# First modulation pieces ahead of the sums of squares, first key norms beside the value products, and modulation matmuls and y transposes tied to program order

## The chip, the cores and the metric

The kernel is one program on one core of a Trainium2 chip. The metric is the device time of one execution in microseconds (us), as the median of several; the profile is that of one execution, taken by the hardware profiler. Names used below: PE is TensorE (matrix products), PEld its weight loads, DVE is VectorE, ACT is ScalarE, POOL is GpSimd, SP is SyncE, whose queue issues the DMAs.

## The reference, cut to what matters

Two blocks of two layers each run over 256 tokens and 256 context tokens of width 2048. The change lies mostly in the first layer of the first block and in the first layer of the second. Every layer modulates its input with vectors that come from a product of a condition with a 2048 x 6144 matrix:

```python
shift_l, scale_l, gate_l = jnp.split((sc @ mod_w[l] + mod_b[l])[:, None, :], 3, axis=-1)
shift_c, scale_c, gate_c = jnp.split(scc @ mod_w[l] + mod_b[l], 3, axis=-1)
```

The first layer is windowed attention: h is x divided by its root mean square (a sum of squares over the 2048 features of each token), scaled and shifted by the modulation, and q, k, v and a gate are products of h with one matrix; each head of q and k is normed, and for the latent tokens rotated, before the scores. The first layer of the second block holds a recurrence over heads of 64, computed in chunks of 64 tokens, whose output y is normed by chunk rows before it is scaled:

```python
mu = jnp.mean(y, -1, keepdims=True)
var = jnp.mean(jnp.square(y - mu), -1, keepdims=True)
yn = ((y - mu) * lax.rsqrt(var + GN_EPS)).reshape(B, T, RWKV_W) * gn_g + gn_b
```

## The kernel before, in words

All activations lie feature by token, 16 blocks of 128 features by 512 tokens (256 context, 256 latent). Products run in split precision: each operand is a high part (`hi`, made by ACT) and a low part (`lo`, the difference, made by DVE), and `mm3` issues three matmuls, hi by hi, hi by lo, lo by hi (lines 368 to 370). Weights stream from memory by `weights`: a DMA of two blocks (`raw`, line 354), then `split` into `whi` (ACT, line 339) and `wlo` (DVE, line 340); after each block of weights it calls `fill`.

`fill` is what sets the order of the side work. It holds generators with a rate each; at every call it adds the rate and runs as many steps as are owed. Two generators exist. `mod_steps` is the modulation: a step takes one loaded piece of modulation weights (`mraw`, 1 MB, by `mod_load`) and multiplies it with the conditions into one PSUM bank (`mv`, line 270); after a batch of pieces the sums are transposed back (line 286) and the bias is added (line 293). `mod_open` gives it a pool with a number of buffers and a rate for the stage, `mod_close` ends that, and `need` runs steps until the named column groups are done. `PACE` gives the rates, by stage: 0.3 in the windowed attention (swa), 0.5 in its output stage (x1), 0.2 in the second layer (mla), 0 in its output stage (x2), 0.25 in the recurrence stage (even), 0.5 in its output stage (x3). The other generator is `rwkv_units`: 16 units (8 head pairs by two directions), up to four at a time, one step of each active unit per `fill`.

The order in which each engine finally issues its instructions is made at compile time by a scheduler: it goes through the instructions in the order in which the program traced them, with priorities, and lets an instruction go ahead of others when it reckons its operands to be ready and an engine to be free. `keep_in_program_order(ins)` takes that freedom away: it puts an instruction behind the instruction traced before it on the same engine, in order of issue alone, with no wait. In `mod_steps` it stands on all matmuls of a piece but the first, so that a piece stays together, while its first matmul may move.

The first stage, in `tile_network`, goes so: x is loaded in four DMAs, ACT squares it and DVE sums the squares into `acc`; three modulation loads are issued; `rms_spread` makes the sums over features on PE (`tok_sums`, line 480), the power -1/2 on POOL (line 472) and a spread over partitions on PE (line 490). Then for each pair of feature blocks the modulation columns are run (`need`), the blocks of h are made by `put_h` (lines 510 to 516), and key products (`keys`, accumulators `kb`) and value products (`values`, banks `vp`) follow in pieces from the list `todo`. `gqa` comes after that stage: it loads norm rows, sine and cosine tables, then norms the four key tiles `kb[t]` (`head_norm`, lines 627 to 649, `late` and `feat` for the transposes to features, line 660, at most `VL` = 2 kept waiting) and starts the query products, whose four accumulators are those of the keys.

At the end of a unit, `rwkv` norms `y` (lines 1465 to 1476), transposes it in two banks of four transposes (`yt`, line 1487), and scales it.

Of the kernel before, what the change touches and what calls it, by code (L numbers as in the profile page):

```python
# [18 lines left out]
P = 128  # L19
# [41 lines left out]
VQ = 3  # L61
# [57 lines left out]
class Net:  # L119
# [129 lines left out]
    def mod_steps(self):  # L249
        nc = self.nc  # L250
        for i in range(4):
            if i % 2 == 0:
                self.conditions(i // 2)
            mod, cs = self.mod[i], self.cs
            for gs in MOD_BATCHES if i else MOD_FIRST:
                pb = self.bank("mv")
                half = isinstance(gs[0], tuple)
                nq, nk, cols = (2, 8, 256) if half else (4, 4, 512)
                for n, g in enumerate(gs):
                    for q in range(nq):  # L260
                        while len(self.mod_ahead) < (self.mod_pool[1] - 1 if self.mod_pool and self.mod_loads else 0):
                            self.mod_load()
                        if not self.mod_ahead:
                            self.mod_load()
                        raw = self.mod_ahead.pop(0)

                        for kk in range(nk):
                            k, j = nk * q + kk, kk % 4
                            with self.tc.high_priority(None if kk else 0):
                                mm = nc.tensor.matmul(  # L270
                                    pb[32 * j : 32 * j + 32, :cols], cs[:, 32 * k + 30 - 2 * n : 32 * k + 62 - 2 * n],
                                    raw[:, kk, :], start=(n == 0 and k < 4), stop=(n == len(gs) - 1 and k >= KD - 4),
                                    tile_position=(0, 32 * j),
                                )
                                if kk:
                                    self.tc.keep_in_program_order(mm)
                        self.mod_wait = MOD_LAG
                        yield
                ev = self.t512("ev", cols=cols)
                nc.scalar.copy(ev, pb[:, :cols])  # L280
                for _ in range(MV_LAG):
                    yield
                p2 = self.bank("mv2")
                c, nb = 2 * len(gs), cols // P
                for j in range(nb):
                    nc.tensor.matmul(
                        p2[:, c * j : c * j + c], ev[:, j * P : (j + 1) * P], self.sel[:, :c], start=True, stop=True
                    )
                for n, g in enumerate(gs):
                    o = g[0] * 4 + g[1] * 2 if half else g * 4  # L290
                    bias = self.v("mod_b", i * 48 + o, nb).unsqueeze(2).broadcast_to([P, nb, 2])
                    pv = p2[:, : nb * c].rearrange("p (j n c) -> p j n c", j=nb, c=2)[:, :, n, :]
                    nc.vector.tensor_tensor(mod[:, o : o + nb, :], pv, bias, op=ALU.add)
                    self.mod_done.add((i, g))
                    if half and g[1]:
                        self.mod_done.add((i, g[0]))
                yield
# [175 lines left out]

    def tok_sums(self, srcs, tiles, rhs):

        pb = self.bank("sums")
        w = rhs.shape[-1]
        for t in range(tiles):
            for n, src in enumerate(srcs):
                self.nc.tensor.matmul(  # L480
                    pb[:, t * w : (t + 1) * w], src[:, t * P : (t + 1) * P], rhs,
                    start=(n == 0), stop=(n == len(srcs) - 1),
                )
        return pb

# [12 lines left out]

    def rms_spread(self, acc, tiles):
        pb = self.tok_sums([acc], tiles, self.ones)  # L500
        rs = self.small(4, "rs")
# [183 lines left out]

    def gqa(self, w, windowed, kb, v=None):
        nc, I, h = self.nc, self.I, self.h
# [4 lines left out]
        with self.tc.tile_pool(name=pre, bufs=1) as ph:  # L692
            pt = v[2] if v else ph
            self.load_rows(pt, [pre + "_q", pre + "_qs", pre + "_k", pre + "_ks"] + (["sink"] if windowed else []))
            tq = self.rope_tables(pt, I[pre + "_cos"], I[pre + "_sin"], pre + "_q", pre + "_qs", P, pre + "q")
            tk = self.rope_tables(pt, I[pre + "_cos"], I[pre + "_sin"], pre + "_k", pre + "_ks", P, pre + "k")
            if windowed:
# [5 lines left out]
                nc.vector.tensor_copy(idr, self.ident)  # L703
            kh, kl = [pt.tile([P, 4, NT], F32R, name=n + pre) for n in ("kh", "kl")]
            vh, vl = v[:2] if v else [ph.tile([P, 4, 512], F32R, name=n + pre) for n in ("vh", "vl")]

            late = []

            def norm(t, ps, dst, tabs, g, base):

                rope = None if t < 2 else (tabs[0][:, t - 2, :], tabs[1][:, t - 2, :])
                q = self.head_norm(ps, 4, P, gain=self.row(g), rope=rope)
                s = slice(t * P - base, (t + 1) * P - base)
                late.append((q, 4, P, dst[0][:, :, s], dst[1][:, :, s]))

            def feat():
                if late:
                    self.to_feat(*late.pop(0))

# [6 lines left out]
            def q_job(g):  # L726
# [3 lines left out]
                for t in toks:  # L730
                    norm(t, banks[t], qs[g], tq, pre + "_q", q0)
                    if len(late) > QLATE[windowed]:
# [10 lines left out]

            for t in range(4):
                norm(t, kb[t], (kh, kl), tk, pre + "_k", 0)
                if v and len(late) > VL:
                    feat()
            if not v:
                vb = {}
# [5 lines left out]
            for n, _ in enumerate(q_job(0)):  # L755
                if v and n < 4 * VQ and n % VQ == VQ - 1:
                    feat()
# [434 lines left out]
    def rwkv(self, ph, b, d, pads, lora, yscr, sums):  # L1192
# [289 lines left out]
        for c0 in (0, 1):  # L1482
            pb = self.bank("yt")
            for n in range(4):
                c = 2 * n + c0
                src = y[:, c : c + 2, :].rearrange("p c t -> p (c t)") if c < NCH - 1 else yw
                nc.tensor.transpose(pb[:, n * P : (n + 1) * P], src, self.ident)
            pv = pb.rearrange("p (n t) -> p n t", n=4)
# [198 lines left out]
def tile_network(ctx, tc, I, out, dbg=None, stop=9):  # L1687
# [11 lines left out]
    with tc.tile_pool(name="x0", bufs=1) as px:  # L1699
# [7 lines left out]
        for _ in range(3):  # L1707
            N.mod_load()
        pr = N.rms_spread(acc, 4)
        rr = px.tile([P, NT], F32, name="rr0")  # L1710
# [13 lines left out]
        def values(g):  # L1724
# [11 lines left out]
            for t in range(4):  # L1736
# [13 lines left out]
                yield  # L1750

        kb = {}
        kgen = keys(kb)
        todo = []
        for g, u in ((g, u) for g in range(4) for u in range(2)):
# [16 lines left out]
            if u:  # L1772
                todo += [values(g)] * 16
        owed = 0.0
# [7 lines left out]
    N.dump("h0", h[0].bitcast(F32))  # L1782
    put_o = N.gqa(I["swa_in"], True, kb, (vh, vl, pV))
    pv.close()
# [33 lines left out]
    with tc.tile_pool(name="x2", bufs=1) as px:  # L1818
        xn = px.tile([P, KD, NT], F32, name="x2")
        N.more(px, XX[1], RX[3])  # L1820
        N.mod_open(px, 3, PACE[3])
        N.need(1, range(12))
# [26 lines left out]
        N.mm_feat(I["ev_lora"][0], h, KD, 256, LAT, [b[:, LAT] for b in lb])  # L1849
        N.mod_close()  # L1850
        N.dump("x2", xn)
# [210 lines left out]
```

## Time and profile before

| | us |
|---|---|
| median of 3 runs | 3263.63 (3262.27 to 3267.89) |
| the profiled execution, its time | 3252.14 |
| the profiled execution, its span (first to last instruction) | 3250.0 |
| mean granted TensorE clock in it | 0.981 |
| PE busy | 3080.6 (95%) |
| DVE busy | 2101.4 (65%) |
| ACT busy | 1481.1 (46%) |

Times of instructions are counted from the start of the span. A clock of 1.00 is 2.4 GHz, 0.50 is 1.2 GHz; a mean between them says that a stretch holds some of each. An engine that is idle costs time only where it is the one that everything else waits for.

### The profile page before, as it was taken

The page shows a single profiled execution, that of the slowest core. Times are in us where ns is not written, and L with a number is a line of the kernel's source. Part 1 is how long each engine was busy: PE and PEld are TensorE (multiplying, and loading weights), DVE is VectorE, ACT ScalarE, POOL GpSimd, SP SyncE. Part 2 cuts the span into 40 slices and gives each one's busy share as a digit, 9 for nine tenths or more (in the row PEclk, how much of TensorE's full clock was granted, in tenths as well). Part 3 has the DMA queues.
Part 4 walks back from the last instruction along what each step waited for, and adds up shares of the span by engine and source line. Part 5 has one row for each costly group of instructions (what it writes and reads, how often), then busy time and mean ns, then how long its engine had stood idle before and what let it go on. Part 6 is the DMA issues. An engine that isn't in the chain of part 4 may idle for free. (4 is left out here: it accounts for less than half of the span.)

```text
span 3250.0 us, 53765 instructions
## 1 busy us (share of the span) xinstructions
PE 3080.6 (95%) x20018; PEld 2399.4 (74%) x20018; DVE 2101.4 (65%) x4663; ACT 1481.1 (46%) x3237; POOL 347.7 (11%) x536
## 2 busy tenths in 40 slices
PE   6999999989988999999999999999999999899997
PEld 4667777767777878897776666766767768678887
DVE  3356455543476666665887788778877555857766
ACT  3324444442376666653334333433434424646664
POOL 0000000000001111000122222222221101200000
PEclk8999999999999999999999999999999999999999
DMA  8843444358654656766434434334445474443454
GB/s 309 319 158 130 149 139 153 137 185 283 232 168 136 229 195 230 258 224 204 142 95 150 127 110 133 98 105 148 124 130 161 165 269 141 161 143 130 143 180 152
DMA packets 270773, 556.10 MB, mean 171 GB/s; under 512 B 122928, under 2 KB 150704, under 8 KB 244912
## 3 DMA queue, kind: packets, MB, share of 16 engines
q1 hardware_dynamic: 270512, 552.68, 51.0%
q8 instruction: 157, 2.57, 0.3%
q14 instruction: 104, 0.85, 0.1%
HBM read 517.46 MB, written 35.13 MB: 170 GB/s over the span
## 5 line engine op out<-in xcount | busy, mean ns | idle before, releaser
L340 DVE TENSOR_TENSOR wlo<-raw,whi 128x512 fp32r<-128x512 f32 (+2 forms) x1000 | 660.5, 668 | 545.7 <-ACT whi L339 510.8
L368 PE MATMUL a<-hhi,whi 128*128 128x512 f32 (+1 forms) x2752 | 972.4, 354 | 16.6 <-ACT whi L339 12.1
L339 ACT CAST whi<-raw 128x512 fp32r<-128x512 f32 (+2 forms) x1000 | 592.7, 599 | 800.9 <-PE a L369 467.5
L369 PE MATMUL a<-hlo,whi 128*128 128x512 f32 (+1 forms) x2752 | 947.2, 345 | 0.3 <-DVE hlo L461 0.3
L370 PE MATMUL a<-hhi,wlo 128*128 128x512 f32 (+1 forms) x2752 | 939.8, 347 | 3.4 <-DVE wlo L340 3.1
L368 PEld LDWEIGHTS a<-hhi,whi 128*128 128x128 f32 x2752 | 524.9, 191 | 124.1 <-ACT whi L339 43.3
L370 PEld LDWEIGHTS a<-hhi,wlo 128*128 128x128 f32 x2752 | 522.1, 191 | 61.7 <-DVE wlo L340 8.4
L369 PEld LDWEIGHTS a<-hlo,whi 128*128 128x128 f32 x2752 | 525.6, 191 | 48.7 <-issue 4.5
L472 POOL TENSOR_TENSOR rs<-st,mhalf 128x4 f32<-128x4 f32 (+3 forms) x109 | 149.0, 1367 | 1660.8 <-DVE st L469 1632.9
L368 PE MATMUL a<-whi,hhi 128*128 128x512 f32 (+1 forms) x672 | 262.3, 401 | 15.9 <-ACT sq L629 6.4
L369 PE MATMUL a<-wlo,hhi 128*128 128x512 f32 (+1 forms) x672 | 264.6, 394 | 1.5 <-DVE wlo L340 1.3
L370 PE MATMUL a<-whi,hlo 128*128 128x512 f32 (+1 forms) x672 | 261.2, 391 | 0.0
L270 PE MATMUL mv<-mraw,cs 128*32 128x512 f32 (+1 forms) x1792 | 212.3, 562 | 16.2 <-DMA mraw<-mod_w 10.9
L1443 POOL TENSOR_SCALAR SD<-SV,DL 64x64 f32<-64x64 f32 x224 | 123.8, 553 | 462.5 <-DVE SV L1454 446.2
L368 PEld LDWEIGHTS a<-whi,hhi 128*128 128x128 f32 x672 | 127.1, 191 | 61.5 <-ACT whi L339 12.8
L369 PEld LDWEIGHTS a<-wlo,hhi 128*128 128x128 f32 x672 | 128.9, 192 | 33.7 <-DVE wlo L340 7.7
L370 PEld LDWEIGHTS a<-whi,hlo 128*128 128x128 f32 x672 | 128.5, 191 | 27.5 <-issue 2.9
L581 ACT ACTIVATE pr<-sc,nm 128x512 f32<-128x512 f32 (+1 forms) x128 | 81.0, 633 | 91.9 <-DVE nm L578 66.4
L1437 DVE COPY Rp<-chain 64x64 f32<-64x64 f32 x256 | 56.7, 221 | 72.1 <-PE chain L1434 69.1
L572 DVE TENSOR_REDUCE mx<-sc 128x1 f32<-128x512 f32 (+1 forms) x128 | 78.9, 617 | 37.1 <-PE sc L782 16.1
L1460 ACT COPY y<-chain 64x64 f32<-64x64 f32 x256 | 52.7, 206 | 109.1 <-PE chain L1457 98.4
L1446 ACT COPY SV<-chain 64x64 f32<-64x64 f32 x128 | 26.5, 207 | 161.5 <-DVE SV L1445 153.5
(379 smaller groups left out, 4678.9 us busy)
## 6 DMA issues: line engine op xcount, KB each, us to landing
mraw<-mod_w SPq DMA_DIRECT2D x160, 1024.0 KB, 4.9
raw<-od_in SPq DMA_DIRECT2D x88, 512.0 KB, 3.6
raw<-swa_in SPq DMA_DIRECT2D x72, 512.0 KB, 3.5
mraw<-mod_h SPq DMA_DIRECT2D x32, 1024.0 KB, 6.1
raw<-ev_rkv SPq DMA_DIRECT2D x64, 384.0 KB, 4.0
raw<-ev_in SPq DMA_DIRECT2D x48, 512.0 KB, 4.0
raw<-swa_out SPq DMA_DIRECT2D x40, 512.0 KB, 5.6
raw<-ev_out SPq DMA_DIRECT2D x40, 512.0 KB, 3.7
```

The lines of the kernel that those rows point to most:

```text
L270: mm = nc.tensor.matmul(pb[32 * j : 32 * j + 32, :cols], cs[:, 32 * k + 30 - 2 * n : 32 * k + 62 - 2 * n], raw[:, kk, :], start=(n == 0 an ...
L339: nc.scalar.copy(whi, raw)
L340: nc.vector.tensor_tensor(wlo, raw, whi.bitcast(F32), op=ALU.subtract)
L368: mm(out, ah, bh, start=first, stop=False, skip_group_check=shared)
L369: mm(out, ah, bl, start=False, stop=False, skip_group_check=shared)
L370: mm(out, al, bh, start=False, stop=last, skip_group_check=shared)
L472: self.nc.gpsimd.tensor_tensor(dst, stv, mv, op=ALU.pow)
L572: nc.vector.reduce_max(mx, sc, axis=AX.X)
L581: nc.scalar.activation(pr[:, :n], sc, AF.Exp, scale=scale, bias=nm, accum_out=sm)
L1437: nc.vector.tensor_copy(Rp[half[hh]], blk(0, hh))
L1443: nc.gpsimd.tensor_scalar(SD[r_], SV[r_, hh, c, :], DL[r_, c : c + 1], None, ALU.mult)
L1460: nc.scalar.copy(y[r_, c, :], blk(3 * P, hh))
```

## The change

- **Modulation pieces.** Before `rms_spread` in the first stage two modulation steps are run (`N.advance("mod", 2)`), and the matmuls of the sums of squares are kept behind them in program order (`behind=True`).
- **Key norms.** What `gqa` did first (rows, tables, key tiles, the closures that norm and transpose) moves into a new function `heads`. For the windowed attention it is called in the first stage, ahead of the loop over feature blocks, and the four key norms are interleaved with the value products of the last feature group, one ahead of every four steps. `gqa` then takes the normed keys and the values as `done`. For the other attention the order stays.
- **Paced modulation.** Where the rate is above zero the first matmul of each piece, too, is kept in program order.
- **y transposes.** The first of each four is kept in program order.
- **x2.** `mod_open` and `mod_close` go from this stage (its rate was 0).

```diff
+                        paced = "mod" in self.side and self.side["mod"][1] > 0
                         for kk in range(nk):
...
-                                if kk:
+                                if kk or paced:
                                     self.tc.keep_in_program_order(mm)
...
-    def tok_sums(self, srcs, tiles, rhs):
+    def tok_sums(self, srcs, tiles, rhs, behind=False):
...
-                self.nc.tensor.matmul(
+                mm = self.nc.tensor.matmul(
...
+                if behind:
+                    self.tc.keep_in_program_order(mm)
...
+    def heads(self, pt, windowed):
+        I, pre = self.I, "swa" if windowed else "od"
+        self.load_rows(pt, [pre + "_q", pre + "_qs", pre + "_k", pre + "_ks"] + (["sink"] if windowed else []))
+        tabs = {
+            n: self.rope_tables(pt, I[pre + "_cos"], I[pre + "_sin"], f"{pre}_{n}", f"{pre}_{n}s", P, pre + n) for n in "qk"
+        }
+        keys = [pt.tile([P, 4, NT], F32R, name=n + pre) for n in ("kh", "kl")]
+        late = []
+        def norm(t, ps, n, dst, base):
+            rope = None if t < 2 else (tabs[n][0][:, t - 2, :], tabs[n][1][:, t - 2, :])
+            q = self.head_norm(ps, 4, P, gain=self.row(f"{pre}_{n}"), rope=rope)
+            s = slice(t * P - base, (t + 1) * P - base)
+            late.append((q, 4, P, dst[0][:, :, s], dst[1][:, :, s]))
+        def feat():
+            if late:
+                self.to_feat(*late.pop(0))
+        return keys, late, norm, feat
...
-            for t in range(4):
-                norm(t, kb[t], (kh, kl), tk, pre + "_k", 0)
-                if v and len(late) > VL:
-                    feat()
-            if not v:
+            if not done:
+                for t in range(4):
+                    norm(t, kb[t], "k", (kh, kl), 0)
...
-                nc.tensor.transpose(pb[:, n * P : (n + 1) * P], src, self.ident)
+                tr = nc.tensor.transpose(pb[:, n * P : (n + 1) * P], src, self.ident)
+                if not n:
+                    self.tc.keep_in_program_order(tr)
...
-        pr = N.rms_spread(acc, 4)
+        N.advance("mod", 2)
+        pr = N.rms_spread(acc, 4, behind=True)
...
+        hd = N.heads(pV, True)
+        def key_norms():
+            for t in range(4):
+                hd[2](t, kb[t], "k", hd[0], 0)
+                if len(hd[1]) > VL:
+                    hd[3]()
+                yield
...
-        kgen = keys(kb)
+        kgen, kn = keys(kb), key_norms()
...
-                todo += [values(g)] * 16
+                v = values(g)
+                todo += ([kn] + [v] * 4) * 4 if g == 3 else [v] * 16
...
-    put_o = N.gqa(I["swa_in"], True, kb, (vh, vl, pV))
+    put_o = N.gqa(I["swa_in"], True, kb, (hd, (vh, vl)))
...
         N.more(px, XX[1], RX[3])
-        N.mod_open(px, 3, PACE[3])
         N.need(1, range(12))
...
         N.mm_feat(I["ev_lora"][0], h, KD, 256, LAT, [b[:, LAT] for b in lb])
-        N.mod_close()
```

## Rows read from the trace of the kernel before

**Rows 1.** The page: an engine's busy time; modulation loads, KB each, us to landing.
```profile
PE 3080.6 (95%) x20018; PEld 2399.4 (74%) x20018; DVE 2101.4 (65%) x4663; ACT 1481.1 (46%) x3237; POOL 347.7 (11%) x536
...
mraw<-mod_w SPq DMA_DIRECT2D x160, 1024.0 KB, 4.9
```

**Rows 2.** Waits of PE: us in total, times, longest us.
```profile
PE sums L480 <- DVE acc L1539: 20.8, 1, 20.8
...
PE yt L1487 <- DVE y L1476: 11.1, 4, 4.1
PE mv L270 <- DMA mraw<-mod_w: 10.9, 6, 3.7
```

**Rows 3.** Timeline of the start: start, us, instruction, idle before and its releaser.
```profile
20.75 1.84 PE L480 MATMUL sums<-ones,acc 128*128 128x2 f32 x8 [20.75 <-DVE acc L1539]
...
25.06 5.00 PE L270 MATMUL mv<-mraw,cs 128*32 128x256 f32 x48
...
31.68 1.07 PE L270 MATMUL mv<-mraw,cs 128*32 128x256 f32 x16 [1.62 <-DMA mraw<-mod_h]
...
35.02 1.58 ACT L510 ACTIVATE hf<-xr,mod,s 128x256 f32<-128x256 f32 x3 [1.83 <-DVE s L551]
...
38.18 2.07 PE L368 MATMUL a<-whi,hhi 128*128 128x512 f32 x4 [1.64 <-ACT whi L339]
```

**Rows 4.** SP's issues; DMA busy tenths from 12 to 30 us; landing of early loads.
```profile
4.24 24.85 SPq L244 DMA_DIRECT2D mraw<-mod_h  x5
...
DMA  9999797979798999989791000000000000097589
...
mraw<-mod_h SPq DMA_DIRECT2D x5, 1024.0 KB, 13.3
```

**Rows 5.** Windows around the handover: length; busy us (instructions) by engine; granted clock, DMA.
```profile
161.50:175.78 14.28, 14.28 (x74) 9.41 (x72) 7.43 (x14) 4.65 (x8) 0.00 (x0) 1.00 0.44 143
175.78:186.94 11.16, 7.30 (x24) 3.29 (x23) 9.97 (x26) 3.60 (x6) 3.03 (x3) 0.69 0.37 109
186.94:200.00 13.06, 13.06 (x60) 10.68 (x59) 9.30 (x16) 3.76 (x7) 1.01 (x1) 1.00 0.53 190
```

**Rows 6.** Timeline of DVE in the handover.
```profile
178.56 0.87 DVE L649 SCALAR_TENSOR_TENSOR hr<-hr,rs,row_swa_k 128x128 f32<-128x128 f32 x3
...
183.54 0.68 DVE L340 TENSOR_TENSOR wlo<-raw,whi 128x512 fp32r<-128x512 f32 x1
```

**Rows 7.** Timeline at the entries of x1, x2 and x3.
```profile
714.03 1.06 PE L270 MATMUL mv<-mraw,cs 128*32 128x512 f32 x8 [3.63 <-DMA mraw<-mod_w]
...
717.78 2.18 ACT L339 CAST whi<-raw 128x512 fp32r<-128x512 f32 x4 [6.62 <-DMA raw<-swa_out]
...
1326.47 0.37 SPq L246 DMA_DIRECT2D mraw<-mod_w  x1
...
1332.09 1.07 PE L270 MATMUL mv<-mraw,cs 128*32 128x512 f32 x8 [3.74 <-DMA mraw<-mod_w]
1333.40 2.18 ACT L339 CAST whi<-raw 128x512 fp32r<-128x512 f32 x4 [4.61 <-DMA raw<-mla_out]
...
2611.35 7.35 SPq L246 DMA_DIRECT2D mraw<-mod_w  x2
...
2625.42 0.50 PE L368 MATMUL a<-hhi,whi 128*128 128x512 f32 x1 [3.19 <-ACT whi L339]
```

**Rows 8.** Timeline of two bursts of the even stage.
```profile
1819.43 1.93 PE L270 MATMUL mv<-mraw,cs 128*32 128x512 f32 x8
...
2129.53 1.75 PE L1487 MATMUL yt<-ident,y 128*128 128x128 f32 x7 [3.81 <-DVE y L1476]
2129.95 1.41 DVE L1415 TENSOR_TENSOR tt<-inv,t 64x512 f32<-64x512 f32 x2
...
2131.51 1.06 PE L1420 MATMUL x<-tt,Z 32*32 32x32 f32 x32
...
2145.78 0.51 ACT L1460 COPY y<-chain 64x64 f32<-64x64 f32 x2 [1.88 <-PE chain L1457]
```

More of the change, by code (lines that the diff above doesn't have):

```diff
@@ L497, in head_spread, with rms_spread @@
         return self.tok_spread(lambda t: e[:, t * P : (t + 1) * P], 4)
-    def rms_spread(self, acc, tiles):
-        pb = self.tok_sums([acc], tiles, self.ones)
+    def rms_spread(self, acc, tiles, behind=False):
+        pb = self.tok_sums([acc], tiles, self.ones, behind)
         rs = self.small(4, "rs")
@@ L683, in rope_tables, with gqa @@
         return t1, t2
-    def gqa(self, w, windowed, kb, v=None):
+    def heads(self, pt, windowed):
[15 more added lines that the diff above has]
+        return keys, late, norm, feat
+    def gqa(self, w, windowed, kb, done=None):
         nc, I, h = self.nc, self.I, self.h
@@ L692, in gqa @@
         with self.tc.tile_pool(name=pre, bufs=1) as ph:
[L693 to L696, printed above, removed]
+            (kh, kl), late, norm, feat = done[0] if done else self.heads(ph, windowed)
             if windowed:
@@ L703, in gqa @@
                 nc.vector.tensor_copy(idr, self.ident)
[L704 to L718, printed above, removed]
+            vh, vl = done[1] if done else [ph.tile([P, 4, 512], F32R, name=n + pre) for n in ("vh", "vl")]
             self.more(ph, SEX if windowed else 2, RX[0] if windowed else RX[4])
@@ L730, in q_job @@
                 for t in toks:
-                    norm(t, banks[t], qs[g], tq, pre + "_q", q0)
+                    norm(t, banks[t], "q", qs[g], q0)
                     if len(late) > QLATE[windowed]:
@@ L755, in gqa @@
             for n, _ in enumerate(q_job(0)):
-                if v and n < 4 * VQ and n % VQ == VQ - 1:
+                if done and n < 4 * VQ and n % VQ == VQ - 1:
                     feat()
```

## Prediction

> **What bounds the kernel now.** I read the page's engine line first: TensorE (PE) is busy 95% of the span [rows 1], so this program is a stream of matmuls, and a change that adds or removes no matmul can only move what is left, some 170 us in which PE stands still, and the time that PE spends at the lower of its two clocks. The second view is the list of PE's waits, longest first in total [rows 2]: three of its entries lie where the diff works, 20.8 us before the first sums of squares, 11.1 us in four waits of the y transposes, and 10.9 us in six waits of modulation matmuls for their weights. Together they are 42.8 us, 1.3% of the span, and the reader should see at once that this is a ceiling: a wait that goes is worth only the distance to the next thing that is late. So for each I read the timeline around it and asked what comes next.
>
> **Part 1, two modulation pieces ahead of the sums of squares.** The cost of the start is read in [rows 3]. The sums start at 20.75 us, when the last square is added. The 64 matmuls of the first modulation column pair then take 25.06 to 32.75, the last 16 after a wait for the fourth load, and only then, at 35.02, can the first h tile be scaled, so the first product of the main stream runs at 38.18. The loads show why the fourth is late [rows 4]: five loads of 1 MB are queued from 4.24 us, the three that fit the buffers run until 21.9 us (22 busy slices of 0.45 us after 12.0), and then the DMA engines stand idle until about 27.3, because a buffer is free only after a third of the 48 matmuls. The median time to landing is 13.3 us; as two of the five are late ones, that is the first load: 4.24 + 13.3 = 17.5. At 1 MB in some 2.4 us the second lands near 19.9, the third at 21.9.
> After the change the first two loads' matmuls stand ahead of the sums in PE's order. Each is a third of 5.00 us, 1.67 us: 17.5 to 19.2, and 19.9 to 21.6. The pinned sums start at 21.6 in place of 20.75, 0.85 us late, and everything behind them (the power on POOL, the spread, the scaled row) is late by that. The third piece then fits while POOL works. The fourth load is issued at 19.2 instead of some 27, follows the third in the DMA engines and lands near 24.3 to 26.5; the upper end holds the row, cosine and sine loads of the attention, nine transfers that `heads` now issues here, past which the fourth load may have to move. The fourth piece ends near 27.5. It ended at 32.75, so the first h tile comes 5.2 us earlier. Nothing is added, and up to 60 us PE keeps waiting for loads that all moved with the buffers, so I take 5.0; bounds 0 (the nine transfers and the next buffers eat it) and 6.0.
> The Trainium skill speaks against this part: "TensorE: Matmul & The Clock Gate", section "Step-by-step: what each phase is for", says that only weight loads are pulled ahead, matmuls stay in program order. By it a pinned sum waits for both loads whatever the data does, and if the second load landed 5 us later than worked out above, the part would bring nothing. No row here shows a matmul passing another.
>
> **Part 2, key norms beside the value products.** The views are the windows around the handover [rows 5] and DVE's rows in it [rows 6]. From 175.78 to 186.94, 11.16 us, PE issues 24 instructions; in the stretch behind, 60 take 13.06, 0.22 each, so the 24 are worth 5.2 us and 6.0 us are lost, some of it as clock (mean granted 0.69 there, 1.00 on both sides). The four accumulators of the keys are read out by the norms, one after another, and the first low half of the next weights comes from DVE at 183.54. Moved ahead, the norms' DVE work goes under the value products. Its size, with 0.68 us for an operation over 128 x 512 (the low half at 183.54) and 0.29 for a scaling of one head (0.87 for three): a copy, a reduction and four scalings for two of the token tiles, 2.5 each, a copy, a reduction and four full operations for the other two, 4.1 each, 13.2 us together, and two transposed low halves: 14.6 us. DVE has 7.43 us of its own in the 14.28 us before the handover. 7.4 + 14.6 = 22.0 does not fit into 14.28; DVE then ends the norms near 161.5 + 22.0 = 183.5, the very time of the first low half now. What saves the gain is that accumulators come free earlier (only copy and square must run, not the whole norm), that the products with the high half need no DVE, and that DVE idles between a norm's steps. If the low halves are queued behind all norms the gain is 1, if they slip between them 6.0. I take 4.0. The four feature transposes per tile are the same work, earlier. The table loads are those of part 1; their old place on SP's queue was hidden, PE being full there.
>
> **Part 3, paced modulation pinned, the x2 stage without modulation.** Of the six waits, two are at the entry of x1, 3.63 us at 714.03 and the one behind it, one (3.74 us) at the entry of x2 [rows 7]. At x1 the next product needs weights that are cast at 717.78, after a wait of 6.62 us for their own load: take the modulation away and PE stands there all the same. I give it 0 (bounds 0 and 3.6). At x2 the load of 1 MB issued at 1326.47 stands ahead of the weights, which are cast only at 1333.40. The change drops this load here (the step moves into the next stage, at the same 1.07 us of PE): 1 MB at the 0.4 MB/us of the start is 2.5 us, which I take (bounds 0 and 3.74). At the entry of x3 SP sits 7.35 us at a modulation load that waits for a buffer; a weight load stands behind it in the queue, and PE waits 3.19 us at 2625.42. With the pieces held at their place, that load should stand later in the queue: I take 2.0, bounds 0 and 3.2.
> The price: a piece that used to run in a stall, where PE had nothing else, now runs in its place. The piece at 1819.43 is such a one [rows 8]; it takes 1.93 us at the low clock there. There are 160 loads and as many pieces [rows 1]. I count about one stalled microsecond each for one or two of them, 1.5 us; bounds 0 and 20 (one in eight). Part 3: 2.5 + 2.0 - 1.5 = 3.0.
>
> **Part 4, y transposes pinned.** At 2129.53 the transposes end a wait of 3.81 us [rows 8]. What is late next: the next matmuls on PE (x, 2131.51) need `tt`, which DVE writes from 2129.95 to 2131.36. PE would stand there until 2131.4 with or without the transposes, and they, 1.75 us in the stall now, would come after it. So the wait changes its name. I take 0; bounds -6 (five bursts at 1.1 us) and +8 (most of the 11.1 us comes back, where DVE is ahead). Behind the transposes stand ScalarE's scalings of y and the sum on DVE, and the next unit's first copy into the single `y` buffer, which here comes at 2145.78, 14 us after the transposes: a few microseconds do no harm there.
>
> **Sum.** 5.0 + 4.0 + 3.0 + 0 = 12.0 us. The profiled execution took 3252.14 us (span 3250.0 and 2.1 around it), so its like would take 3240.1; it lies 11.5 us below the median of 3263.63, and against the median, which is what is compared, I predict 3251.6.
>
> **Rivals.** (a) *All of it comes back*, parts 1 and 2 at their upper bounds, x2 and x3 too, nothing paid for the pins, and the y transposes find a DVE that is ahead: 6.0 + 6.0 + 3.74 + 3.2 + 8 = 26.9, so 3236.7. For it: the stall at the handover holds low clock [rows 5], which would go too. Against it: DVE's rows in parts 2 and 4. Chance 0.16, from 3230 to 3244. (b) *The waits change their names*: the start is held by the next buffers, DVE ends the norms no earlier, x3's queue stays: 2 + 1 + 1 = 4 us, 3259.6; chance 0.24, 3257 to 3270. This is also the case that the change does not do what it says. (c) *Slower: the filler is taken out of the stalls.* One mechanism: pieces that ran in gaps of PE now run in its full stretches, at 1.07 us each. Without the price the sum is 13.5 us; 13 of the 160 pieces eat it, from 19 on the kernel is slower by 0.2%, and at 30 the time is 3263.6 - 13.5 + 32.1 = 3282. For it: the span less PE's busy time and the first 20.75 us leaves some 149 us of gaps after the start [rows 1, 3], and a piece that is ready early runs in one. Against it: PE is 95% busy, so most pieces already run among products. Chance 0.14.
>
> **How the numbers follow.** The forecast holds 0.46, by itself from 3244 to 3257. Under 0.2% (6.5 us) a measurement of this kernel tells little from no change: faster is forecast and (a), 0.62; same 0.24; slower 0.14. For 8 in 10 I go from 3237, leaving out half of (a), to 3268, leaving out (c).
>
> **What would show it.** Right: the sums start 21 to 22, the first h tile near 30 and the first main product near 33; no idle DMA after the third load; the stretch from values to queries 4 us shorter with clock over 0.8; no modulation load at the entry of x2 and weights cast near 1331 minus the shift; PE's wait at x3 under 1.5 us. Wrong: sums later than 23, a new wait for `wlo` or for a value bank in the value products, pieces of modulation after which nothing is shorter, or in the even stage waits for `tt` and `wlo` that exceed those of y now.

## The result and the profile after

The changed kernel takes 3294.4 us (3293.0 to 3296.4), the kernel before beside it 3265.8: ratio 1.009, 95% interval 1.0076 to 1.0104, 28.6 us slower where 12 us faster was forecast. The profiled execution takes 3294.15 us, its mean granted clock is 0.976 (0.981 before). The page's engine line, which answers to [rows 1]:

```profile
PE 3097.7 (94%) x20018; PEld 2415.3 (73%) x20018; DVE 2104.8 (64%) x4663; ACT 1480.4 (45%) x3237; POOL 350.6 (11%) x536
```

With the same 20018 matmuls PE is busy 17.1 us longer. To find the place I compared when SP first issues the weights of each stage. The timeline of SP at the first weights of the even stage and of the stage behind it, in the kernel before and then in the changed one:

```profile
1445.94 0.33 SPq L354 DMA_DIRECT2D raw<-ev_rkv  x1
...
2537.92 0.33 SPq L354 DMA_DIRECT2D raw<-ev_out  x1
```

```profile
1432.36 3.59 SPq L355 DMA_DIRECT2D raw<-ev_rkv  x2
...
2578.09 0.33 SPq L355 DMA_DIRECT2D raw<-ev_out  x1
```

Up to the even stage 13.6 us are gained, in it 53.7 lost (1145.7 for 1092.0), behind it nothing changes by more than 3. That makes 42 us, as between the two profiled executions, and not the 28.6 of the medians: the profiled execution of the kernel before, 3252.14 us, is the fastest of that kernel on record (the next takes 3252.96). Against the stage of e8 and e12 below, which leave it alone (1098.1 and 1106.5 us), the loss is 39 to 48. The window of the even stage, first of the kernel before, then of the changed one (length; busy us and instructions of PE, PEld, DVE, ACT, POOL; clock; DMA):

```profile
1446.00:2538.00 1092.00, 1049.94 (x7654) 761.32 (x7653) 845.70 (x1955) 420.80 (x1051) 222.82 (x404) 0.98 0.44 136
```

```profile
1432.00:2578.00 1146.00, 1072.69 (x7661) 779.81 (x7659) 849.29 (x1957) 421.49 (x1051) 227.00 (x404) 0.96 0.43 130
```

Two things grow: PE's idle time, length less busy, from 42.1 to 73.3, and PE's busy time for the same work. The second is clock. Cut into windows of 10 us (110 before, 115 after) and summed as 2 x (1 - granted clock) x length, PE is at the lower level, 1.2 GHz, for 40.8 us before and 95.6 after. Half of the 54.8 is lost, 27.4, and with the 31.2 of idle time that is 58.6 for 53.7 found. It is 5 us too much because the two overlap: PE is busy in 76.0 of the 95.6 us and in 37.0 of the 40.8, and its busy time in the stage grew by 22.5 (1049.9 to 1072.4), not by 27.4. The Trainium skill ("TensorE: Matmul & The Clock Gate", section "HAM oscillation — how this bites in real kernels") prices time at the lower clock at half of it; here that comes out to within 5 us, 27.4 for 22.5.

PE's waits in that window of the changed kernel (total, times, longest):

```profile
PE a L371 <- DVE wlo L341: 35.4, 8, 8.7
PE chain L1447 <- DVE Rp L1446: 4.7, 7, 2.2
...
PE yt L1496 <- ACT Z L1420: 2.5, 3, 0.9
```

The 11.1 us of the y transposes [rows 2] are gone, and 35.4 us for low halves of the weights stand in their place. One of them, on PE's timeline:

```profile
1803.72 1.15 PE L1405 MATMUL inv<-t,Z 64*64 64x64 f32 x32
1813.47 1.65 PE L371 MATMUL a<-hhi,wlo 128*128 128x512 f32 x3 [8.60 <-DVE wlo L341]
1815.05 1.94 PE L271 MATMUL mv<-mraw,cs 128*32 128x512 f32 x8
1816.91 1.50 PE L1496 MATMUL yt<-ident,y 128*128 128x128 f32 x7
...
1818.46 0.69 PE L1429 MATMUL x<-tt,Z 32*32 32x32 f32 x32
1819.31 1.16 PE L1295 MATMUL gram<-AQ,BK 64*128 64x128 f32 x8 [0.16 <-ACT yf L1507]
```

I call such a stretch, in which PE has few products to run, a burst: DVE works for the recurrence units for 16 us without a break (from 1796.89) and casts no low half until 1812.86. Behind the low product stand the piece, the transposes, `x` and `gram`; the piece, 1.07 us at full clock, takes 1.94.

### The profile page after: what moved, and what is told of

It is laid out like the page before. It is cut to its first block, busy times and chain, and to the rows that moved or that the text cites. A ratio compares the mean times of both kernels' runs of the same rounds, so it can differ in the third digit from the quotient of the medians.

```text
span 3292.4 us, 53788 instructions
## 1 busy us (share of the span) xinstructions
PE 3097.7 (94%) x20018; PEld 2415.3 (73%) x20018; DVE 2104.8 (64%) x4663; ACT 1480.4 (45%) x3237; POOL 350.6 (11%) x536
## 5 line engine op out<-in xcount | busy, mean ns | idle before, releaser
L371 PEld LDWEIGHTS a<-hhi,wlo 128*128 128x128 f32 x2752 | 527.5, 193 | 96.2 <-DVE wlo L341 43.1
L369 PEld LDWEIGHTS a<-whi,hhi 128*128 128x128 f32 x672 | 125.9, 190 | 58.1 <-ACT whi L340 12.8
L371 PEld LDWEIGHTS a<-whi,hlo 128*128 128x128 f32 x672 | 127.6, 190 | 27.4 <-issue 3.3
L271 PEld LDWEIGHTS mv<-mraw,cs 128*32 128x32 f32 x1792 | 40.0, 111 | 88.4 <-issue 47.5
```

The source lines that it names most:

```text
L271: mm = nc.tensor.matmul(pb[32 * j : 32 * j + 32, :cols], cs[:, 32 * k + 30 - 2 * n : 32 * k + 62 - 2 * n], raw[:, kk, :], start=(n == 0 an ...
L369: mm(out, ah, bh, start=first, stop=False, skip_group_check=shared)
L371: mm(out, al, bh, start=False, stop=last, skip_group_check=shared)
```

## The experiments

The experiments come in four groups; beside them the kernel before took 3260.6 to 3262.4 us. What they show of the even stage stands in one table. Stage is the time between the two issues of SP above, idle is stage less PE busy, low is the time at 1.2 GHz summed as above, pieces are those of the stage's 51 modulation pieces with under 1.2 us of products between 2.5 us before their start and 2.5 us after their end, so those that run in bursts.

| kernel | median us | stage | idle | low | pieces in bursts |
|---|---|---|---|---|---|
| before | 3263.6 | 1092.0 | 42.1 | 40.8 | 9 |
| changed | 3294.4 | 1145.7 | 73.3 | 95.6 | 1 |
| e1, transposes free | 3275.2 | 1117.1 | 55.8 | 71.8 | 0 |
| e2, even pieces free | 3253.9 | 1099.2 | 42.7 | 54.6 | 9 |
| e3, both free | 3250.9 | 1100.6 | 43.1 | 54.4 | 9 |
| e4, before with the y pin | 3259.6 | 1098.1 | 41.3 | 54.6 | 9 |
| e5, units first, transposes free | 3241.0 | 1081.1 | 38.1 | 17.2 | 5 |
| e6, pieces behind the high product | 3284.7 | 1138.0 | 56.9 | 105.8 | 0 |
| e7, no pins | 3242.4 | 1095.1 | 43.3 | 44.2 | 9 |
| e8, before with part 1 | 3258.4 | 1098.1 | 44.3 | 47.6 | 9 |
| e9, units first, both free | 3240.3 | 1085.9 | 38.1 | 23.8 | 8 |
| e10, units first, pins in even alone | 3231.3 | 1087.0 | 40.6 | 20.6 | 5 |
| e11, units first, y pin | 3252.5 | 1095.4 | 49.7 | 10.2 | 3 |
| e12, before with part 2 | 3252.0 | 1106.5 | 38.6 | 74.8 | 9 |
| e13, e3 without even pieces | 3244.1 | 1091.1 | 60.5 | 95.4 | - |
| e14, e13 with pins | 3258.0 | 1101.3 | 67.3 | 98.8 | - |
| e15, units first, no pins | 3235.5 | 1093.9 | 37.7 | 48.2 | 8 |

Stage less idle less half of low is 1025 to 1041 us in every row with its pieces, so most of what differs is how long PE stands and how long it is slow. Counting of the slow time only what PE is busy in, the rows are 1030 to 1041. The count in the last column moves with its limits; with limits of 0.8 to 2.0 us of products and 2.0 to 3.0 us of distance no other kernel holds fewer than the changed one, e1 and e6. It tells these three from the rest and doesn't rank the rest. Single profiles scatter: kernels that leave this stage alone (before, e8, e12) show 1092 to 1106 us, so verdicts go by medians.

**First group: which pin?**

e1 takes out the y pin, e2 the pin of the even stage's pieces, e3 both; e4 puts the y pin alone on the kernel before.

```diff
# e1, e3
-                if not n:
-                    self.tc.keep_in_program_order(tr)
# e2, e3
-                        paced = "mod" in self.side and self.side["mod"][1] > 0
+                        paced = "mod" in self.side and self.side["mod"][1] > 0 and self.side["mod"][1] != PACE[4]
```

> The changed kernel with the y transposes free again, everything else as changed. Theory Y (the y pin makes the loss: the transposes now stand behind the low products of the main stream, and what follows them stands there too): the even stage goes back to about 1100 us from 1153, the time falls from 3294 to about 3250, some 14 us under the kernel before. Theory M (the paced pin of the modulation pieces makes the loss in the even stage, since they no longer fill the waits there): stays near 3294.

> The changed kernel with the modulation pieces of the even stage free again, the y pin kept. Theory Y: near 3290, the long waits for the low half of the weights stay. Theory M: near 3250.

> The changed kernel with both pins of the even stage taken out; pinned pieces stay in swa, x1, mla and x3. Both theories: the even stage as before, 3250 to 3252. If it stays above 3265 the loss is neither pin's but comes from what the earlier stages hand over (load order, the step moved out of x2).

> The kernel before with the y pin alone. Theory Y: slower by 40 to 54 us, about 3305 to 3320, with waits for the low half of over 6 us in the even stage. Theory M: within 5 us of 3265. A loss of half that size: the two pins work together.

Ratios: e1 1.004 (1.0026 to 1.0054), e2 0.998 (0.997 to 0.9989), e3 0.9971 (0.9957 to 0.9984), e4 0.9994 (0.9983 to 1.0005). Theory Y falls with e2 and e4, and theory M holds but for e1, which it put near 3294 (the 1153 us in e1's expectation is 1145.7 by the marks used here). The pin of the pieces is the loss: it costs 24.3 us without the y pin (e1 - e3) and 40.5 with it (changed - e2). In the profiles 16.5 of the 24.3 lie in the stage; 4.6 lie ahead of it, where e1 and e3 have the same code, which is scatter. The y pin by itself costs nothing that can be measured, on free pieces (e2 - e3, 3.0; e4, -2.8), yet 19.2 on pinned ones (changed - e1; 15.9 if each is taken against the kernel before that ran beside it). The two are not independent. The order in which the program traces PE's matmuls says why they can't be: of the 51 pieces of the stage 50 are traced right behind a product with a low half, and of the 16 first transposes 12 right behind a piece. Pinned, they form a chain: low half, product, piece, transposes.

The same burst in e3 shows what a free piece does:

```profile
1805.12 0.63 PE L1496 MATMUL yt<-ident,y 128*128 128x128 f32 x4 [2.08 <-DVE y L1485]
1806.06 1.06 PE L271 MATMUL mv<-mraw,cs 128*32 128x512 f32 x8 [0.31 <-DMA mraw<-mod_w]
...
1808.30 0.69 PE L1429 MATMUL x<-tt,Z 32*32 32x32 f32 x32 [0.48 <-DVE tt L1424]
1808.92 1.96 PE L1295 MATMUL gram<-AQ,BK 64*128 64x128 f32 x16
...
1813.82 1.65 PE L271 MATMUL mv<-mraw,cs 128*32 128x512 f32 x8
...
1826.43 1.20 PE L371 MATMUL a<-hhi,wlo 128*128 128x512 f32 x2
```

Two pieces, the transposes, `x` and `gram` run ahead of the low product, which is issued only at 1826.43. DVE's low half is even later here (1824.18), and PE doesn't wait for it.

**Second group: the chain, or the filler?** Theory C says that the first link of the chain is the loss, theory F that the pieces are missed in the bursts.

```diff
# e5, on e1 (fill: the units' step is traced ahead of the piece)
-        for n in list(self.side):
+        for n in sorted(self.side, reverse=True):
# e6, on the changed kernel: hi_mm is the high-half product ahead of the low-half one
+                            even = paced and not kk and "rwkv" in self.side
+                            with self.tc.high_priority(None if kk else 0), (
+                                self.tc.issue_after(self.hi_mm.ins) if even else nullcontext()
+                            ):
...
+                                if kk or (paced and not even):
...
-        mm(out, ah, bl, start=False, stop=False, skip_group_check=shared)
+        self.hi_mm = mm(out, ah, bl, start=False, stop=False, skip_group_check=shared)
# e7, on e3
+                        paced = False
# e8, on the kernel before
+        N.advance("mod", 2)
+        pr = N.rms_spread(acc, 4, behind=True)
```

> Edit: the changed kernel with the y transposes free, pieces pinned, and in the even stage the recurrence units' step is traced ahead of the piece, so that a piece stands behind a unit's matmul in place of behind a product with the low half of the weights. Theory C (chain: a pinned piece stands behind a low-half product, which waits for DVE's low half, and what shares its place stands there with it): the even stage falls from the 1117.1 us of the kernel with free transposes and pinned pieces to about the 1100.6 us of the one with both free, whole time about 3254 (3248 to 3260). Theory F (filler: a pinned piece no longer runs in a stall, wherever it is pinned, and costs its own 1.07 us among the products): it stays near 1117, whole time 3268 to 3282.

> Edit: the changed kernel complete, y transposes pinned; only, in the even stage the first matmul of a piece is kept behind the product with the high half that comes one before the low-half product, so that the chain low half, product, piece, transposes loses its first link and nothing else. Theory C: the 35.4 us of waits for the low halves in the even stage go (under 8 left), the stage falls from 1145.7 to 1098 to 1108, whole time 3251 to 3262. Theory F: the pieces stay near their places, the stalls too; the stage stays over 1130, whole time over 3278. A third view, Q, that the transposes pinned in order cost by themselves once the pieces are where they are: 1117 to 1130, whole time 3266 to 3280.

> Edit: neither pieces nor y transposes are pinned anywhere; what stays of the change is the two pieces ahead of the sums, the key norms beside the value products and the output stage without modulation. It prices the pins outside the even stage. Theory C says nothing of them. If they brought part of the 13.6 us that the stages before the even one lost, the time goes from the 3250.9 of the kernel with those pins alone to 3254 to 3260, the low-rank stage before the even one starting some 5 us later. If they cost something there or at the last stage's entry (waits of 4.4 us at 2664.98 against 3.2 before), it falls to 3244 to 3249.

> Edit: the kernel before with part 1 alone, two modulation pieces ahead of the sums of squares, which stand behind them in program order. The prediction gave it 5.0 us (bounds 0 and 6): the first issue of the attention's weights at 24.8 in place of 29.1, the attention's output stage about 4.4 us earlier, the whole 3257 to 3259 where the kernel before has 3262.4. A rival: the later buffers take it back by the end of the first attention, as the changed kernel lost there 9.2 us at the handover and only 5.2 at 430 us: then under 2 us are left.

e5 0.9941 (0.9923 to 0.996), e6 1.0076 (1.0061 to 1.0091), e7 0.995 (0.9935 to 0.9965), e8 0.9991 (0.9978 to 1.0003). Neither theory foresaw e5: C wanted 3248 to 3260 us, F 3268 to 3282, and it took 3241.0. F's "wherever it is pinned" is wrong: behind a unit's matmul a pin costs nothing. e6 is the sharp one for C. PE's waits in its even stage, and under them the first of e1's:

```profile
PE a L374 <- DVE wlo L344: 9.6, 3, 8.7
PE yt L1499 <- DVE y L1488: 5.2, 2, 2.9
```

```profile
PE a L371 <- DVE wlo L341: 9.6, 3, 8.7
```

The waits for low halves fall from 35.4 to 9.6, nearly as theory C said, and the kernel is still 24 us slower than before; e1 has the same 9.6 and is 12.8 slower. Of the 25.8 us that go only 16.4 show as less idle time, since other waits grow, and the time at the lower clock grows by 10.2, to 105.8. So that wait, the longest line of the list, was mostly a symptom, and theory C, which wanted 3251 to 3262, fell. What e6 shares with e1 and the changed kernel, and not with the others, is that at most one piece in 51 runs in a burst, not 3 to 9. In e5 pieces are pinned too, but behind a unit's matmul; 5 stay in the bursts (e9's expectation counted 9), and nothing is lost.

**Third group: what a pin is tied to, and the parts alone.**

```diff
# e9, on e3; e11, on the changed kernel
-        for n in list(self.side):
+        for n in sorted(self.side, reverse=True):
# e10, on e5
-                        paced = "mod" in self.side and self.side["mod"][1] > 0
+                        paced = "mod" in self.side and self.side["mod"][1] == PACE[4]
# e12: the kernel before with heads, key_norms and the new todo alone
```

> Edit: as the kernel with the units' step traced ahead of the piece and y transposes free, but with the pieces of the even stage free again. After the second group theory F is put more sharply: what counts is how many pieces run in the bursts, where few products lie near (9 of 52 in the kernel before, 1 in the changed one, 1 with free transposes, 1 behind the high-half product, 9 behind the units' matmuls), and how much clock the bursts hold. By F the stage stays within 6 us of the 1081.1 with pieces behind the units' matmuls, whole time 3235 to 3249. Rival K: it is the pin behind a unit's matmul that keeps a piece for the burst, a free one runs when its load lands; then the stage goes back to some 1100, whole time 3250 to 3258.

> Edit: the units' step ahead of the piece, transposes free, pieces pinned in the even stage alone and free in all others. From the second group the pins outside the even stage bring nothing net (the stage before the even one starts 14.0 us early without any pin, 13.4 with them). If that holds, the time is that of the same kernel with pins everywhere, 3241, within 5 us; if the pins in the first output stage bring the 4 us that its interval showed, 3245 or more.

> Edit: the changed kernel complete with one difference, the units' step is traced ahead of the piece. Then 44 of the 51 pieces stand behind a unit's matmul, and the first transpose of all 16 units stands directly behind a product with a low half; in the changed kernel 12 of the 16 stood behind a pinned piece, and that piece behind such a product; with free pieces the 12 stood behind a piece that may run early. Theory L (the y pin costs where what it is tied to is itself held behind products): the even stage is 20 to 30 us longer than the 1081.1 with free transposes, 1101 to 1111, whole time 3261 to 3271. Rival N (only the lost filler counts, the y pin by itself nothing): it stays at 1076 to 1090, whole time 3236 to 3250.

> Edit: the kernel before with part 2 alone, key norms beside the value products, no pin and no pieces ahead of the sums, the output stage with its modulation. The prediction gave it 4.0 us (bounds 1 and 6): 3256 to 3259 where the kernel before has 3261, the attention's output stage starting 4 us earlier. Rival: DVE's work is only moved, and the queries lose it: under 1 us at the output stage. By the second group's sum (14.0 us without any pin, 5 of it part 1) it would be up to 8.

e9 0.9934 (0.9909 to 0.9958), e10 0.9901 (0.9875 to 0.9928), e11 0.997 (0.9956 to 0.9985), e12 0.9977 (0.996 to 0.9995). e9 is as fast as e5, so free pieces and pieces behind a unit's matmul do the same: F in its sharper form holds, rival K falls. That the count of pieces in bursts is what matters is shown only so far: it sorts the kernels, and no run moved those pieces alone. Against e3 the trace order alone brings 10.7 us. In e11 all 16 first transposes stand directly behind a low product, and the y pin costs 11.5 us (e11 - e5), between L's 20 and N's nothing. e12 was expected at 3256 to 3259 and took 3252.0. e10 was expected at 3241 and took 3231.3: the pins outside the even stage cost something, and this is the fastest kernel of the case, 0.99% under the one before.

**Fourth group: the price of a piece.** e13 leaves out the matmuls of the modulation in the even stage, e14 does so with both pins, e15 is e7 with the units first.

```diff
# e13, on e3; e14, on the changed kernel
+                            if "rwkv" in self.side and not (n == 0 and k < 4 or n == len(gs) - 1 and k >= KD - 4):
+                                continue
```

> Edit: the kernel with free transposes, in which the modulation's matmuls of the even stage are left out, but for the first four and the last four of each bank (180 of 204 are left out, 45 pieces' worth; the loads stay, the later modulation vectors are incomplete). At 1.07 us a piece 45 pieces are 48.2 us of PE. Theory F (pinned pieces cost their own time among the products, free ones fill bursts and cost less): 3275.2 - 48.2 = 3227 (3220 to 3234), so that a free piece costs (3250.9 - 3227) / 45 = 0.53 us. Rival P (a free piece costs its own 1.07 us as well, a pinned one some 0.5 more wherever it stands): 3250.9 - 48.2 = 3203 (3196 to 3210).

> Edit: the changed kernel, y transposes pinned, with the same 180 matmuls left out. The first transpose of most units then stands directly behind a product with a low half. Theory L (the y pin costs by what it is tied to): 11 to 20 us more than the same without the pin. Rival N (it costs only where a piece stands between): within 5 us of the same without the pin.

> Edit: the two pieces ahead of the sums, the key norms beside the value products, the output stage without modulation, no pin on pieces or transposes anywhere, and the units' step traced ahead of the piece. Where pieces are free everywhere but in the even stage, behind the units' matmuls, it was 3231.3; where they were free in the even stage and pinned elsewhere 3240.3. If only the trace order counts in the even stage and the pins elsewhere cost the 9 us: 3228 to 3236. If the pin behind a unit's matmul is worth something: 3237 to 3246.

e13 0.995 (0.9927 to 0.9974), e14 0.9988 (0.9977 to 1.0), e15 0.9916 (0.9901 to 0.9931), 3235.5 us, just inside its first range: in the even stage the pin behind a unit's matmul is worth little, and the pins elsewhere cost. Rival P (3203) falls; F was right in direction and too timid: e13 takes 3244.1, not 3227. Left out, 45 pieces' worth of matmuls save 6.8 us against free pieces, 0.15 us a piece, and 31.1 against pinned ones (e1), 0.69 a piece. A free piece is nearly free: the intervals of e13 and e3 overlap, so 6.8 can't be told from none. e13's even stage says where the 48.2 us of matmuls went (compare e3's window, second):

```profile
1434.00:2526.00 1092.00, 1031.56 (x7322) 780.13 (x7321) 843.62 (x1953) 422.98 (x1049) 231.55 (x404) 0.96 0.45 136
```

```profile
1433.00:2533.00 1100.00, 1056.94 (x7655) 766.06 (x7653) 845.99 (x1955) 421.44 (x1051) 222.49 (x404) 0.98 0.44 135
```

17.4 us more idle time, 41.0 us more at the lower clock. e14 - e13 is 13.9 us: the y pin costs where no piece stands between, too. The transposes are then tied to products, and PE's waits for low halves are 17.1 us in e14 and 6.1 in e13.

## Why the prediction was wrong

**The start (part 1) came in part.** The timeline of the changed kernel, PE, ACT and SP, which answers to [rows 3] and [rows 4]:

```profile
20.39 1.93 PE L271 MATMUL mv<-mraw,cs 128*32 128x256 f32 x16 [0.46 <-DMA mraw<-mod_h]
22.25 1.87 PE L482 MATMUL sums<-ones,acc 128*128 128x2 f32 x8
...
35.17 1.20 PE L369 MATMUL a<-whi,hhi 128*128 128x512 f32 x4 [2.55 <-ACT whi L340]
```

```profile
32.01 1.58 ACT L514 ACTIVATE hf<-xr,mod,s 128x256 f32<-128x256 f32 x3 [1.43 <-DVE s L555]
```

```profile
20.36 0.33 SPq L684 DMA_DIRECT2D t2swaq<-swa_sin  x1
...
23.89 0.83 SPq L244 DMA_DIRECT2D mraw<-mod_h  x2
```

The sums start at 22.25 (21.6 forecast), right behind the second piece, though DVE's last addition to `acc` ended at 20.94. The rule that the prediction cites from the Trainium skill ("TensorE: Matmul & The Clock Gate", section "Step-by-step: what each phase is for"), that matmuls stay in program order, agrees with these rows. The first h tile comes at 32.01 (30 forecast), since the nine transfers of `heads` stand ahead of the fourth load, which is issued at 23.89, not 19.2; the first product at 35.17 is 3.0 us early. Of the 5.0 forecast, SP shows 4.3 to 5.2: by so much earlier the attention's first weights are issued in the kernels that hold parts 1 and 2. PE shows less: its first product comes at 35.17 to 37.61 in them, at 33.84 in e8 without the nine transfers, and at 38.18 to 39.91 where the old start stands (before, e4, e12). Alone (e8) its profile is 5.3 us ahead at the even stage; the median, 2.2, can't be told from none.

**The handover (part 2) came.** The window over the new handover, which answers to [rows 5]:

```profile
166.00:178.00 12.00, 10.29 (x52) 7.28 (x51) 11.38 (x21) 5.70 (x10) 1.01 (x1) 1.00 0.04 12
```

1.71 us idle at full clock, where 6.0 were lost at 0.69: 4.3 us for the 4.0 forecast. Alone (e12) the whole kernel gains 8.9 us (1.6 to 13.0 by its interval).

**The stages behind (part 3, gains) were mis-sized, both ways.** At x2 the modulation load is gone, and PE stands at the same place for a weight: the second entry below, against 3.74 at 1332.09 [rows 7]. 2.5 was forecast; the stage's interval is 0.8 us longer in the changed kernel and 1.8 shorter in e7, so little is left. At x3 I gave 2.0 for a wait of 3.19; it is 4.41 now, third entry. The modulation load was to stand later in SP's queue, and it stands there as before, for 7.86 us where it was 7.35 (last entry). At x1 the wait only changes its name, as forecast.

```profile
701.16 0.50 PE L369 MATMUL a<-hhi,whi 128*128 128x512 f32 x1 [3.67 <-ACT whi L340]
```

```profile
1320.27 0.58 PE L369 MATMUL a<-hhi,whi 128*128 128x256 f32 x1 [3.46 <-ACT whi L340]
```

```profile
2664.98 0.80 PE L369 MATMUL a<-hhi,whi 128*128 128x512 f32 x1 [4.41 <-ACT whi L340]
```

```profile
2650.87 7.86 SPq L246 DMA_DIRECT2D mraw<-mod_w  x2
```

Together parts 1, 2 and x2 without a pin (e7) bring 18.3 us, for 11.5 forecast. The changed kernel is 28.6 slower, so all pins together cost 46.9, each kernel taken against the kernel before that ran beside it.

**The price of the pins is the step that failed.** It read: "I count about one stalled microsecond each for one or two of them, 1.5 us; bounds 0 and 20". Measured, the pin of the even stage's pieces costs 24.3 us. Rival (c) had the mechanism, the filler taken out of the stalls, and 3282 for its time, but its argument against itself ("most pieces already run among products") decided, and it was true and no answer: 42 of 51 pieces of the even stage do run among products, and the loss goes with the 9 others. Two things were wrong in its size. A piece was priced at its own 1.07 us; a burst that loses its filler and the work behind it loses time at both ends, 12.7 us of idle and 17.4 us at the lower clock in e1 against e3. And how many pieces ran in bursts could have been counted in the kernel before, where they bunch (1866.6, 1872.9 and 1881.2, then none until 1965.8): [rows 8] show one, the stage holds 9. How the clock falls in such a place shows in three windows of 2.5 us of the changed kernel: PE is busy 1.10 us in the first, and the granted clock goes from 1.00 to 0.50.

```profile
1610.00:1612.50 2.50, 1.10 (x8) 0.93 (x8) 2.47 (x7) 0.58 (x2) 0.53 (x1) 1.00 0.33 98
1612.50:1615.00 2.50, 2.25 (x12) 1.86 (x11) 2.44 (x7) 0.00 (x0) 0.00 (x0) 0.64 0.19 21
1615.00:1617.50 2.50, 2.50 (x8) 2.06 (x8) 0.59 (x1) 0.00 (x0) 0.00 (x0) 0.50 0.74 240
```

**The y pin (part 4) was right alone and wrong in the sum.** The 0 us is borne out by e4, and not by the mechanism, "So the wait changes its name": there the four waits stay with the y transposes, 11.1 us as before; the piece traced ahead of them is free. But the parts were added as if independent. What a pin costs depends on what stands ahead of the pinned matmul: a free piece, nothing; a product with a low half, 11.5 to 13.9 us; a piece that is itself pinned behind such a product, 15.9 to 19.2. The forecast named who stands behind the transposes, and never what they stand behind. One of its signs of being wrong is what came: in the even stage waits for `wlo`, 35.4 us, that exceed those of y, 11.1.

The pins in the other stages cost 4.8 to 9.6 us by the medians (e9 - e15, e3 - e7, e5 - e10). In which of those stages the most is lost stays open: the stages' intervals differ by 2 to 5 us, and the first issue that marks them moves with SP's queue. Open, too, is why tracing the units first gains another 6.9 to 10.7 us with free transposes (e7 - e15, e3 - e9): in e5, e9 and e10 the time at the lower level is 17 to 24 us, in e15 48, and the order differs at many places, of which only the sum was measured.

## What to carry to other kernels

Before pinning filler work to program order, count how much of it runs where the engine has nothing else, and price the pin by what those stretches lose in idle time and clock, not by the filler's own length. Look up what is traced right ahead of each instruction that is pinned: the pin inherits every wait of that one, and two pins in a row make a chain that costs more than each by itself. When a new wait tops the list, take its cause away before believing it, since the same loss may come back under another name.

## What was not expected of the hardware

Leaving 48.2 us of matmuls out of the even stage made it 9.5 us shorter in the two profiles (e13 and e3; 6.8 by the medians): PE's idle time grew by 17.4 us, and its time at 1.2 GHz from 54.4 to 95.4 us, half of which is 20.5. In this stage four fifths of such work is paid back, by the clock as much as by the gap it fills.
